# Gate products beside an RWKV scan without empty steps, and adaLN weights in four column groups

## The chip, the cores and the metric

The kernel runs on one core of a Trainium2 chip, in one launch. The metric is the device time of that launch in microseconds (us): the median of three runs, and beside it one execution that the hardware profiler recorded. The engines are TensorE (PE, with its weight loads PEld), VectorE (DVE), ScalarE (ACT), GpSimd (POOL) and SyncE (SP, which here issues most of the DMAs). All data are float32.

## The reference, cut to what matters

Two layers of a diffusion backbone over 256 context tokens and 512 latent tokens, 1024 wide. In the second layer (the last) only the latent tokens are carried on.

```python
def hybrid_layer(x, ctx, c, c_ctx, ...):
    shift, scale, gate = split(silu(c) @ ada_w + ada_b, 3)       # adaLN: 1024 x 3072, for c and for c_ctx
    p = split_cols(modulate(x, shift, scale) @ in_w, IN_SPLITS)  # one wide projection
    outs = [mla(p) * silu(p[3]),                                 # four mixers, each with its own gate
            rwkv(p) * silu(p[5]),                                # scan over the tokens, both ways
            gqa(p) * silu(p[9]),
            diff_attn(p) * silu(p[13])]
    g = sigmoid(p[14] + merge_b)                                 # 4 x 1024 merge gates: the widest part of in_w
    y = sum(g[i] * (outs[i] @ branch_w[i]) for i in range(4))
    return post_norm(ALPHA * x + gate * (y @ out_w), ln_g, ln_b)

def rwkv_step(S, r, w, k, v, kk, a):                             # per token and head, S is 64 x 64
    S = S * w - (S @ kk) * (kk * a) + v * k
    return S, S @ r
```

## The kernel before

**How a product is made.** Matmuls of the wide projection are made in three float32r passes: a weight block is split into a rounded part and the rest (`w_split`, L280: DMA at L292, the rounded part on ACT at L293, the difference on DVE at L296), and `mm3` (L299, matmul at L303) adds hi·hi, hi·lo and lo·hi. The blocks hold 1024 columns in a pool `wx` of five buffers; a block needs three of them, one for the raw weights and one for each part.

**Stages.** In us of the profiled span: the adaLN of layer 0 (0 to 45); the projections and the three attentions of layer 0 (45 to 592); its RWKV scan beside the gate products (592 to 988); its branch merges (988 to 1112); its output projection, with the last adaLN blocks of layer 1 (1112 to 1215); then the same for layer 1: attention to 1630, scan 1630 to 1965, merges to 2058, output to the end.

**The scan.** `rwkv_scan` (L1077) is a generator whose every step ends in a `yield`. It goes over six groups of two chunks of 64 tokens. `rwkv_prepare` (L1145) makes a group's matrices: products with `wup` and `aup` (L1167), G and the like (L1242, L1254, with DVE's L1246), and then an inverse in levels. A level is one dependent chain over two engines: DVE transposes D into tmp (L1290), 32 matmuls of 32x32 (L1295), DVE scales (L1298), 32 matmuls (L1319), DVE adds to D (L1320). `rwkv_chunks` (L1348) carries the state along (L1364, L1378, L1389, L1399).

**The gate products beside it.** `out_gate` and `late_gate` (through `m_block`) and `merge_gates` (through `t_block`) are a second generator, `rest`. For layer 0 it works on 768 tokens in two cuts of 384, for layer 1 on 512 in one. After every second of eight weight rows a block yields, so a step holds six matmuls of `mm3`. Before a block begins, `take_w` (L492) yields once with no work issued, and again as long as `wbusy` says that another generator is in the midst of a weight block. The gate products end in ACT's tanh (L1442), or in `gate` (L1413), where DVE's L1416 frees the PSUM buffer.

**What sets the order.** PE's order is that in which the program issues (`manual_schedule`); the other engines' orders come from the scheduler's priorities. `beside` (L203) runs the scan and, after each of its steps, as many steps of `rest` as `RATE[l]` (L36) has become due: 2.37 a step for layer 0, 1.3 for layer 1. Ahead of the scan `LEAD[2]` = 6 steps of `rest` are run; what is left of it comes after the scan. A step without work counts like any other.

```python
due = 0.0
for w in first:
    due += rate * (1.0 if w is None else w)
    while due >= 1:
        due -= 1
        next(second, None)
```

**adaLN.** `ada` (L376) multiplies the two conditioning vectors by 1024x3072 weights in six blocks of 512 columns a layer. A block comes in four pieces of 128x1024, each one DMA (L388). A matmul (L392) takes 128 rows of weights as its moving side, and writes 32 rows of PSUM: the row chunk i uses the array's column group i % 4. After the fourth piece ACT copies the sums (L397) and a small product adds up the four groups (L400). Layer 0's blocks 0 to 3 stand at the start; its blocks 4 and 5 and layer 1's 0 to 3 are filler in layer 0's attention; layer 1's 4 and 5 stand in layer 0's output projection.

**The tail.** `rwkv_finish` (L1100) normalizes the scan's output in two head pairs (PE transposes L1119 and L1121, DVE from L1125 to L1142). `merge` (L1447) multiplies each branch by its weights, transposes at L600, and DVE joins the products with the gates (L1480, L1483).

Of the kernel before, what the change touches and what calls it, by code (L numbers as in the profile page):

```python
# [18 lines left out]
DEPTH = 2  # L19
# [15 lines left out]
LEAD = (6, 1, 6)  # L35
RATE = (2.37, 1.3)  # L36
FILL = ((0.7, 0.65, 0.9), (0.5, 0.4, 0.5))
# [116 lines left out]
def _prep(inp):  # L154

    g = {k: np.asarray(v) for k, v in inp.items()}
    f = {}
    f["xin"] = np.concatenate([g["ctx"][0], g["x"][0]], 0)
    f["cc"] = np.stack([g["c_ctx"], g["c"][0]], -1).reshape(8, 128, 2).transpose(1, 0, 2).reshape(128, 16)
    order = [x for j in range(8) for x in (8 + j, j)] + list(range(16, 24))  # L160
    ada = g["ada_w"].reshape(DEPTH, 4, 2, 128, 24, 128)[:, :, :, :, order].reshape(DEPTH, 4, 2, 128, 6, 512)
    f["adaw"] = ada.transpose(0, 3, 4, 1, 2, 5).reshape(DEPTH, 128, 24 * 1024)
    brw = g["branch_w"].reshape(DEPTH, 4, 2, 128, 8, 128).transpose(0, 3, 1, 4, 2, 5).reshape(DEPTH, 128, 32, 256)
# [49 lines left out]
class _Kernel:  # L213
    def __init__(self, ctx, tc, a, out, tap):
# [14 lines left out]
        self.fp = None  # L229
        self.wbusy = False  # L230
        self.flip2 = 0

# [143 lines left out]
    def ada(self, l, ad, pp, pool, blocks, ahead=None):  # L376

        nc = self.nc
        for b in blocks:
            ps = self.P("A")  # L380
            for q in range(4):
                c = (b * 4 + q) * 1024
                if ahead is None:
                    yield from self.take_w()
                    w = self.t(self.fp, [128, 1024], "wf", bufs=2) if self.fp is not None else self.t(self.wp, [128, WCOLS], "wx", bufs=WBUFS)
                else:
                    w = self.t(ahead[0], [128, 1024], "adaw", bufs=ahead[1])
                nc.sync.dma_start(out=w[:, :1024], in_=self.a["adaw"][l][:, c:c + 1024])  # L388
                for k in range(2):
                    i = 2 * q + k  # L390

                    nc.tensor.matmul(ps[32 * (i % 4):32 * (i % 4) + 32], lhsT=self.cc[:, 2 * i:2 * i + 32], rhs=w[:, k * 512:k * 512 + 512],  # L392
                                     start=i < 4, stop=i >= 4)
                self.wbusy = False
                yield
# [96 lines left out]
    def take_w(self):  # L492

        yield
        while self.wbusy:
            yield
        self.wbusy = True
# [1035 lines left out]
def _run_layers(K, only=None):  # L1533
# [18 lines left out]
    for l in range(DEPTH):  # L1552
# [50 lines left out]
        if only == "attn":  # L1603
            return
        K.fp = None
        left = ExitStack()
        xct.close()
# [15 lines left out]
        with K.psum(A=(1, 2), B=(1, 3), C=(1, 2), Y=(1, 1)):  # L1623
# [14 lines left out]
            with mk(f"mg{l}") as K.mp:  # L1638
# [30 lines left out]
                gates_ = {s: K.gate_rows(ad, s) for s in ((1,) if last else (0, 1))}  # L1669
                run(tail)  # L1670
        with K.psum(A=(1, 8)):
            ys = K.out_operands(y, len(qt) * 128)
# [54 lines left out]
```

## Time and profile before

| | us |
|---|---|
| median of three runs | 2113.36 |
| lowest and highest | 2112.68 and 2114.27 |
| profiled execution | 2116.16 |
| its span, from the first to the last instruction | 2114.4 |
| PE busy | 1916.1 (91%) |
| PEld busy | 1579.2 (75%) |
| DVE busy | 1159.4 (55%) |
| ACT busy | 818.3 (39%) |
| POOL busy | 184.6 (9%) |
| mean granted PE clock | 0.958 |

The profiled execution takes 1.8 us more than its span, and 2.8 us more than the median. A float32 matmul leaves two records in the trace, an fp32r matmul one. Matmuls are pipelined and their ends are modelled, so a start to the next start says more than a duration. The gate products (L303 from `wx`) alone are 691.8 us of PE.

### The profile page before, as it was taken

The numbers are of one execution on the slowest core, as the hardware profiler recorded it, in microseconds if no ns is written. First come the engines' busy times: TensorE is split into PE (matmuls) and PEld (weight loads), VectorE is DVE, ScalarE is ACT, GpSimd is POOL, SyncE is SP. The second block draws the span as 40 slices with busy tenths as digits, with TensorE's granted clock in tenths as the row PEclk, the third lists the DMA queues.
The fourth block names the chain that finished last, engine by engine and source line by source line (L and its number), as shares of the span: only waits on it lengthen the run. The fifth ranks groups of instructions, "written<-read, shape, count | busy, mean of one in ns | idle before, by whom it ended". The sixth has DMA issues, their size and how long they took to land. (4 is left out here: it accounts for less than half of the span.)

```text
span 2114.4 us, 45822 instructions
## 1 busy us (share of the span) xinstructions
PE 1916.1 (91%) x19694; PEld 1579.2 (75%) x19694; DVE 1159.4 (55%) x2471; ACT 818.3 (39%) x1649; POOL 184.6 (9%) x303
## 2 busy tenths in 40 slices
PE   6899999988899999999788779999988988989877
PEld 4778868666788888888677577878877766766656
DVE  5554453576434434343778855454785444444677
ACT  3354452565323333232122336463664333332320
POOL 1000000001200000000230110001011000000120
PEclk9899999999899999999999989999999999999989
DMA  7110132220222222224642310101103222222741
GB/s 274 40 31 28 55 91 90 73 69 21 64 84 72 71 72 72 72 78 144 225 145 102 126 36 21 53 31 51 31 21 96 79 77 67 78 71 77 253 151 40
DMA packets 62612, 176.02 MB, mean 83 GB/s; under 512 B 7448, under 2 KB 12232, under 8 KB 62408
## 3 DMA queue, kind: packets, MB, share of 16 engines
q1 hardware_dynamic: 47144, 139.93, 21.0%
q10 hardware_dynamic: 13824, 27.90, 3.7%
q0 software_dynamic: 1440, 5.24, 0.6%
q8 instruction: 155, 2.54, 0.5%
q14 instruction: 49, 0.40, 0.1%
HBM read 145.50 MB, written 27.55 MB: 82 GB/s over the span
## 5 line engine op out<-in xcount | busy, mean ns | idle before, releaser
L303 PE MATMUL ps<-xh,wx 128*128 128x384 f32 (+2 forms) x3096 | 691.8, 369 | 1.5 <-DVE oth L1416 0.6
L303 PEld LDWEIGHTS ps<-xh,wx 128*128 128x128 f32 x3096 | 536.6, 190 | 64.0 <-issue 6.2
L293 ACT ACTIVATE wx<-wx 128x1024 fp32r<-128x1024 f32 (+2 forms) x94 | 98.2, 1045 | 307.3 <-PE ps L303 223.9
L296 DVE TENSOR_TENSOR wx<-wx,wx 128x1024 fp32r<-128x1024 f32 (+2 forms) x94 | 113.7, 1210 | 134.2 <-ACT wx L293 133.5
L649 DVE TENSOR_REDUCE nmax<-ps 128x1 f32<-128x768 f32 (+1 forms) x160 | 134.8, 847 | 64.3 <-PE ps L646 63.3
L571 PE MATMUL ps<-wx,xh 128*128 128x256 f32 (+1 forms) x1200 | 155.4, 288 | 7.7 <-DVE mu L1000 6.7
L571 PEld LDWEIGHTS ps<-wx,xh 128*128 128x128 f32 x1200 | 151.1, 191 | 9.4 <-ACT xc L476 6.8
L303 PE MATMUL ps<-xh,wb 128*128 128x384 f32 (+1 forms) x576 | 133.4, 384 | 27.1 <-DVE th L1482 19.3
L538 PE MATMUL ps<-wx,xh 128*128 128x256 f32 x960 | 140.3, 299 | 12.8 <-DVE oth L1416 6.3
L652 ACT ACTIVATE E<-ps,nmax 128x768 f32<-128x768 f32 (+1 forms) x160 | 130.5, 817 | 47.1 <-DVE nmax L649 42.9
L646 PE MATMUL ps<-qk,qk 128*128 128x384 f32 (+1 forms) x504 | 131.3, 366 | 17.3 <-ACT E L652 16.9
L303 PEld LDWEIGHTS ps<-xh,wb 128*128 128x128 f32 x576 | 108.0, 202 | 49.4 <-DVE th L1482 17.6
L538 PEld LDWEIGHTS ps<-wx,xh 128*128 128x128 f32 x960 | 129.3, 202 | 18.5 <-DVE oth L1416 6.5
L670 ACT ACTIVATE PH<-ps 128x512 f32<-128x512 f32 x156 | 91.4, 597 | 72.4 <-PE ps L668 71.8
L646 PEld LDWEIGHTS ps<-qk,qk 128*128 128x128 f32 x504 | 82.4, 192 | 45.0 <-ACT E L652 29.7
L668 PE MATMUL ps<-cstalways,E 128*128 128x128 f32 x624 | 102.3, 287 | 2.8 <-ACT PH L670 1.6
L1442 ACT ACTIVATE mth<-ps,hmb 128x384 f32<-128x384 f32 (+1 forms) x96 | 58.6, 610 | 118.6 <-PE ps L303 118.2
L693 PE MATMUL ps<-PH,V 128*64 128x256 f32 x624 | 85.7, 402 | 4.3 <-ACT PH L670 4.1
L668 PEld LDWEIGHTS ps<-cstalways,E 128*128 128x128 f32 x624 | 76.7, 147 | 16.8 <-ACT PH L670 4.3
L628 DVE TENSOR_TENSOR qk<-ps,qk 32x256 fp32r<-32x256 f32 (+5 forms) x104 | 59.3, 575 | 43.4 <-ACT qk L627 41.6
L296 DVE TENSOR_TENSOR wx<-wf,wx 128x1024 fp32r<-128x1024 f32 (+2 forms) x34 | 40.0, 1177 | 60.5 <-PE ps L303 33.8
L693 PEld LDWEIGHTS ps<-PH,V 128*64 128x64 f32 x624 | 41.0, 140 | 37.0 <-ACT PH L670 15.1
(325 smaller groups left out, 2799.9 us busy)
## 6 DMA issues: line engine op xcount, KB each, us to landing
wx<-in_inw_dram SPq DMA_DIRECT2D x88, 512.0 KB, 3.7
wf<-in_inw_dram SPq DMA_DIRECT2D x30, 512.0 KB, 3.6
wf<-in_adaw_dram SPq DMA_DIRECT2D x24, 512.0 KB, 3.6
gd<-mth ACTq DMA_DIRECT2D x32, 384.0 KB, 2.4
th<-gd SPq DMA_DIRECT2D x32, 384.0 KB, 3.1
adaw<-in_adaw_dram SPq DMA_DIRECT2D x16, 512.0 KB, 10.2
wx<-in_outw_dram SPq DMA_DIRECT2D x16, 512.0 KB, 6.2
wb<-in_brw_dram SPq DMA_DIRECT2D x32, 256.0 KB, 3.6
```

The source lines that it names most:

```text
L293: nc.scalar.activation(out=hi[:, :n], in_=raw[:, :n], func=AF.Copy)
L296: eng.tensor_tensor(out=lo[:, :n], in0=raw[:, :n], in1=hi[:, :n].bitcast(F32), op=ALU.subtract)
L303: self.nc.tensor.matmul(o, lhsT=w, rhs=x[:, s] if s is not None else x, start=first and p == 0, stop=last and p == 2)
L538: self.nc.tensor.matmul(ps[:, j * n:j * n + n], lhsT=self.xtok(x[k], s), rhs=w, start=k == 0 and p == 0 and j == 0, stop=k == 7 and p == 2 ...
L571: self.nc.tensor.matmul(ps, lhsT=self.xtok(x[k], s), rhs=w[:, c], start=k == 0 and p == 0 and head, stop=k == 7 and p == 2 and (tail or t ...
L628: nc.vector.tensor_tensor(out=lo[r, s], in0=ps[r], in1=hi[r, s].bitcast(F32), op=ALU.subtract)
L646: nc.tensor.matmul(o, lhsT=qt[:n, q], rhs=kt[:n, s], start=i == 0, stop=i == len(passes) - 1)
L649: nc.vector.tensor_reduce(out=nm, in_=v, axis=AX.X if ctx else AX.XY, op=ALU.max, negate=True)
L652: nc.scalar.activation(out=self.halves(e[:, :n], v), in_=v, func=AF.Exp, bias=nm, accum_out=den)
L668: nc.tensor.transpose(pt[:, c:c + 128], e[:, (k0 + k) * 128:(k0 + k) * 128 + 128], self.ident)
L670: nc.scalar.activation(out=hi, in_=pt, func=AF.Copy)
L693: nc.tensor.matmul(po[64 * (kk % 2):64 * (kk % 2) + 64, :n], lhsT=v2(kk), rhs=x[:, s], start=j == 0 and k < 2, stop=j == len(groups) - 1 a ...
```

## The change

Two edits that have nothing to do with each other.

First, a flag `eager` is set from the end of the attention to the output projection of each layer. While it is set, `take_w` does not yield first; it still yields as long as `wbusy` is set. A block of merge gates has 8 steps instead of 9 in layer 0, and 4 instead of 5 in layer 1; all gate products together 278 instead of 312, and 142 instead of 176. The rates go from 2.37 to 2.15 and from 1.3 to 1.08, so that with the scan's 126 steps of weight 277.0 and 142.1 steps are given out (304.6 and 169.8 before).

Second, an adaLN piece of 1024 columns holds four row chunks by 256 columns instead of two row chunks by 512. Each piece is four matmuls of 256 columns, one on each column group, instead of two of 512 on two groups. The layout of the weights in memory follows it. Bytes, DMAs and sums are the same.

```diff
-RATE = (2.37, 1.3)
+RATE = (2.15, 1.08)
...
-    ada = g["ada_w"].reshape(DEPTH, 4, 2, 128, 24, 128)[:, :, :, :, order].reshape(DEPTH, 4, 2, 128, 6, 512)
-    f["adaw"] = ada.transpose(0, 3, 4, 1, 2, 5).reshape(DEPTH, 128, 24 * 1024)
+    ada = g["ada_w"].reshape(DEPTH, 2, 4, 128, 24, 128)[:, :, :, :, order].reshape(DEPTH, 2, 4, 128, 6, 2, 256)
+    f["adaw"] = ada.transpose(0, 3, 4, 5, 1, 2, 6).reshape(DEPTH, 128, 24 * 1024)
...
-        self.wbusy = False
-        self.flip2 = 0
+        self.wbusy = self.eager = False
...
                 nc.sync.dma_start(out=w[:, :1024], in_=self.a["adaw"][l][:, c:c + 1024])
-                for k in range(2):
-                    i = 2 * q + k
-
-                    nc.tensor.matmul(ps[32 * (i % 4):32 * (i % 4) + 32], lhsT=self.cc[:, 2 * i:2 * i + 32], rhs=w[:, k * 512:k * 512 + 512],
-                                     start=i < 4, stop=i >= 4)
+                half = q // 2 * 256
+                for k in range(4):
+                    i = 4 * (q % 2) + k
+
+                    nc.tensor.matmul(ps[32 * k:32 * k + 32, half:half + 256], lhsT=self.cc[:, 2 * i:2 * i + 32],
+                                     rhs=w[:, k * 256:k * 256 + 256], start=q == 0, stop=q == 3)
                 self.wbusy = False
                 yield
...
     def take_w(self):
 
-        yield
+        if not self.eager:
+            yield
         while self.wbusy:
             yield
         self.wbusy = True
...
         K.fp = None
+        K.eager = True
         left = ExitStack()
...
                 run(tail)
+        K.eager = False
         with K.psum(A=(1, 8)):
```

Where a name in the rows below ends in a number, the number tells one buffer from another. The lines of the new kernel are one lower between L232 and L391, and one higher behind.

On PE, in a group's levels in layer 1's scan, before: the last matmuls of a gate block (L303), a level's second half (L1319), and the first half of the next level (L1295) with nothing between them.

```order
L303 MATMUL ps_18390<-xh_13199,wx_18385 128x512
L303 MATMUL ps_18390<-xh_13201,wx_18385 128x512
L303 MATMUL ps_18390<-xh_13199,wx_18386 128x512
L1319 MATMUL ps_18486<-D_18261,tmp_3153_18478 32x32 x32
L1295 MATMUL ps_18525<-tmp_3156_18523,G_3119_18166 32x32 x2
L1295 MATMUL ps_18525<-tmp_3156_18523,G_3120_18167 32x32 x2
```

The same place in the changed kernel.

```order
L302 MATMUL ps_18591<-xh_13147,wx_18587 128x512
L1320 MATMUL ps_18598<-D_18363,tmp_3153_18580 32x32 x32
L302 MATMUL ps_18591<-xh_13172,wx_18586 128x512
L302 MATMUL ps_18591<-xh_13174,wx_18586 128x512
L302 MATMUL ps_18591<-xh_13172,wx_18587 128x512
L302 MATMUL ps_18591<-xh_13198,wx_18586 128x512
L302 MATMUL ps_18591<-xh_13200,wx_18586 128x512
L302 MATMUL ps_18591<-xh_13198,wx_18587 128x512
L1296 MATMUL ps_18640<-tmp_3160_18638,G_3124_18278 32x32 x2
```

Six gate matmuls now stand between the two halves. Before, 13 pairs of scan steps in layer 1 had nothing between them, 75 stretches of gate matmuls held six, 22 twelve and one 72, and 36 gate matmuls came behind the scan; now no pair is empty, 96 stretches hold six, 16 twelve and one 48, and none comes behind the scan. In layer 0, 18 stretches held six matmuls, 58 twelve and 30 eighteen; now none holds six, 95 twelve and 12 eighteen, and behind the scan are 24 in place of 54. Around L1058, L1167 and L1242 ahead of layer 1's scan stood 36, 36 and 72 gate matmuls, now 48, 48 and 48. At eleven of the block ends in layer 1 DVE's split of the next weights comes in its order right ahead of an add or a scaling of the scan.

On PE, at the end of layer 1's scan, before: the output's transposes (L1119, L1121) of `rwkv_finish`, and 36 gate matmuls, of which the first three and the last stand here, ahead of the first merge (L600).

```order
L1119 MATMUL ps_21976<-cstalways_113,YT_17248 128x128 x4
L1121 MATMUL ps_21977<-cstalways_113,ks_17249 128x128 x4
L303 MATMUL ps_21868<-xh_13134,wx_21863 128x512
L303 MATMUL ps_21868<-xh_13136,wx_21863 128x512
L303 MATMUL ps_21868<-xh_13134,wx_21864 128x512
...
L303 MATMUL ps_21926<-xh_13199,wx_21922 128x512
L600 MATMUL ps_22013<-cstalways_113,O_14713 128x128 x4
```

The same place in the changed kernel.

```order
L302 MATMUL ps_21987<-xh_13291,wx_21983 128x512
L1120 MATMUL ps_22072<-cstalways_113,YT_17381 128x128 x4
L1122 MATMUL ps_22073<-cstalways_113,ks_17382 128x128 x4
L601 MATMUL ps_22109<-cstalways_113,O_14809 128x128 x4
L601 MATMUL ps_22118<-cstalways_113,O_14809 128x128 x4
L1113 MATMUL ps_22125<-ks_17382,cstrwkv_17279 128x512
```

The merge's transposes follow the finish's directly. On DVE the steps of the first head pair's finish now alternate with those of the first merge, where they stood ahead of it.

On PE, in layer 0's attention, before: an adaLN piece (`wf`, L392) between the scores (L646), transposes (L668, L600) and another piece.

```order
L646 MATMUL ps_2811<-qk_2450,qk_2414 128x384 x2
L392 MATMUL ps_2783<-wf_2822,cs_118 32x512 x2
L668 MATMUL ps_2826<-cstalways_113,E_2745 128x128
...
L600 MATMUL ps_2835<-cstalways_113,Qs_1997 128x128 x2
L392 MATMUL ps_2783<-wf_2862,cs_118 32x512 x2
```

The same place in the changed kernel.

```order
L647 MATMUL ps_2843<-qk_2482,qk_2446 128x384 x2
L392 MATMUL ps_2815<-wf_2854,cs_118 32x256 x4
L669 MATMUL ps_2860<-cstalways_113,E_2777 128x128
...
L601 MATMUL ps_2869<-cstalways_113,Qs_2029 128x128 x2
L392 MATMUL ps_2815<-wf_2896,cs_118 32x256 x2
```

A piece is four matmuls of half the width, and sometimes the scheduler cuts it in two. The 48 matmuls of 512 columns that are filler in the attention stood in 27 runs (13 of two, 10 of one, 4 of three), 17 of them between 284 and 394 us and 10 between 394 and 440; now 96 matmuls of 256 stand in 29 (15 of four, 6 of three, 2 of two, 4 of one, 2 of five).

## Rows read from the trace of the kernel before

**Rows 1.** Busy by stage: from:to, us, busy (instructions) per engine, granted clock, DMA share, GB/s.
```profile
284.00:394.00 110.00, 109.64 (x787) 85.93 (x786) 41.83 (x82) 44.34 (x96) 7.61 (x7) 1.00 0.29 88
394.00:440.00 46.00, 39.81 (x187) 21.17 (x188) 33.97 (x74) 30.93 (x71) 0.78 (x3) 0.85 0.43 127
592.00:988.00 396.00, 391.03 (x6539) 348.36 (x6536) 156.11 (x325) 123.06 (x260) 18.87 (x47) 1.00 0.23 74
1630.00:1965.00 335.00, 308.68 (x5675) 230.74 (x5674) 150.06 (x306) 110.25 (x229) 19.30 (x43) 0.97 0.25 76
1965.00:2058.00 93.00, 71.37 (x295) 52.32 (x294) 72.17 (x122) 26.57 (x41) 22.50 (x18) 0.93 0.67 221
```

**Rows 2.** PE's waits in layer 1's scan: waited for, us in total, times, longest.
```profile
PE ps L1319 <- DVE tmp L1298: 6.7, 7, 1.9
PE ps L1295 <- DVE tmp L1290: 5.6, 3, 2.4
...
PE ps L303 <- DVE oth L1416: 0.6, 1, 0.6
```

**Rows 3.** PE in time in layer 1's scan: start, us, instruction, records, [idle before].
```profile
1694.67 0.74 PE L1295 MATMUL ps<-tmp,G 32*32 32x32 f32 x64 [2.39 <-DVE tmp L1290]
...
1697.62 3.08 PE L303 MATMUL ps<-xh,wx 128*128 128x512 f32 x12
1700.63 0.75 PE L1295 MATMUL ps<-tmp,G 32*32 32x32 f32 x64
1701.31 1.67 PE L303 MATMUL ps<-xh,wx 128*128 128x512 f32 x6
1702.91 0.75 PE L1319 MATMUL ps<-D,tmp 32*32 32x32 f32 x64
1706.05 0.74 PE L1295 MATMUL ps<-tmp,G 32*32 32x32 f32 x64 [2.39 <-DVE tmp L1290]
```

**Rows 4.** DVE in time under the last wait of the group above.
```profile
1703.87 1.23 DVE L296 TENSOR_TENSOR wx<-wx,wx 128x1024 fp32r<-128x1024 f32 x1 [2.02 <-ACT wx L293]
1705.01 0.41 DVE L1320 TENSOR_TENSOR D<-D,ps 128x256 f32<-128x256 f32 x1
1705.46 0.45 DVE L1290 STREAM_TRANSPOSE tmp<-D 128x256 f32<-128x256 f32 x1
```

**Rows 5.** Busy in two of five stretches of layer 1's scan at half clock.
```profile
1707.40:1710.60 3.20, 3.20 (x9) 2.49 (x8) 0.00 (x0) 0.00 (x0) 0.00 (x0) 0.50 0.22 84
...
1929.30:1932.50 3.20, 3.20 (x70) 2.65 (x62) 0.87 (x2) 0.00 (x0) 0.00 (x0) 0.50 0.69 203
```

**Rows 6.** PE in time in layer 0's attention, at adaLN pieces (L392).
```profile
309.92 1.06 PE L392 MATMUL ps<-wf,cs 128*32 128x512 f32 x6
310.91 1.51 PE L693 MATMUL ps<-PH,V 128*64 128x256 f32 x12
```

**Rows 7.** PE in time between the layers, a dense adaLN block.
```profile
1197.04 1.92 PE L392 MATMUL ps<-wx,cs 128*32 128x512 f32 x16 [1.91 <-DVE ada L404]
```

**Rows 8.** Busy in two stretches, the instructions of L392 alone: PE, PEld, clock, DMA.
```profile
284.00:394.00 110.00, 17.86 (x60) 2.42 (x60) 1.00 0.29 88
394.00:440.00 46.00, 13.40 (x36) 1.74 (x36) 0.85 0.43 127
```

**Rows 9.** PE in time at the head of layer 1's scan.
```profile
1610.62 1.22 PE L1167 MATMUL ps<-wd,wup 64*128 64x128 f32 x8 [4.69 <-DMA kd<-kt]
...
1624.77 1.11 PE L1242 MATMUL ps<-KR,BK 64*128 64x64 f32 x16
```

**Rows 10.** DVE in time at the same place.
```profile
1623.94 0.42 DVE L1222 TENSOR_TENSOR KR<-kkn,P 128x256 f32<-128x256 f32 x1
```

**Rows 11.** PE in time behind layer 1's scan.
```profile
1965.47 8.69 PE L303 MATMUL ps<-xh,wx 128*128 128x512 f32 x36
```

**Rows 12.** Busy in the same 8.5 us and in the first merge behind them.
```profile
1965.50:1974.00 8.50, 8.50 (x39) 6.79 (x38) 5.97 (x19) 2.59 (x4) 0.87 (x1) 1.00 0.96 330
1974.00:1993.00 19.00, 15.41 (x71) 11.13 (x69) 14.04 (x34) 4.95 (x9) 1.92 (x2) 1.00 0.73 234
```

**Rows 13.** Costliest groups: line, engine, shapes, count, busy, mean ns, idle before.
```profile
L293 ACT ACTIVATE wx<-wx 128x1024 fp32r<-128x1024 f32 (+2 forms) x94 | 98.2, 1045 | 307.3 <-PE ps L303 223.9
```

## The prediction, made before the changed kernel was run

> **What bounds the kernel now.** I read the busy time by stage first [rows 1], because an average over stages with different limits says nothing of one edit. The five stages shown are those that the change touches. In the first of them, most of layer 0's attention, TensorE (PE) is busy 109.64 of 110 us: whatever is taken from PE's own work there is taken from the time. In the next 46 us PE has 39.81 at a mean granted clock of 0.85, with VectorE (DVE) at 33.97 and ScalarE (ACT) at 30.93: PE and the softmax chain take turns. The scan of layer 0 beside the gate products is PE's again (391.03 of 396). The scan of layer 1 is not: 308.68 of 335, which leaves 26.3 us of idle PE and a clock of 0.97. In the merges of layer 1 DVE is busy longer than PE (72.17 against 71.37).
>
> Second, who is waited for in layer 1's scan [rows 2]. The two largest are the scan's own small matmuls waiting for DVE between two of its steps; a gate matmul waits once, 0.6 us, and for the buffer of the gate before it, not for weights. Third, one such wait close up [rows 3, 4]. A step's 64 records (L1319) go out, nothing of the gates stands behind them, and the next step (L1295) starts 2.39 us later. In between DVE first finishes the split of the next weights (L296, 1.23), then adds and transposes (L1320, L1290). Where six gate records stand between two steps, PE has 1.60 us of work (1701.31 to 1702.91). The empty steps thus cost most when DVE has a split ahead of the scan's own work.
>
> Fourth, the granted clock. Five waits of 1.6 to 2.4 us in this stage are each followed within 4 us by at least 3.2 us at 0.50, the 1.2 GHz level; two of the five stretches stand in [rows 5]. Six other waits of 1.1 to 2.4 us are not followed by one (the 2.39 us before 1694.67 in [rows 3] is the nearest), so the loss does not go with the wait's length alone.
>
> **The change part by part.** *The adaLN pieces.* In the attention the products of 512 columns on 32 of the array's columns stand in 27 runs between other matmuls, most of one piece. A run of three matmuls (six records, since one float32 matmul leaves two) has 0.99 us from its start to the next start [rows 6], and eight matmuls spread on all four column groups take 1.92 [rows 7]. So matmuls on different groups lie beside each other, and the time is that of the fullest group: 0.96 for 512 columns. A piece of two matmuls uses two groups only and pays 0.96; a piece of four matmuls of 256 columns uses all four and should pay 0.48. The new order has 29 runs, two of them with a fifth matmul that repeats a group. I take 0.55 for a run (0.48, and 0.07 for an entry that a shorter run hides less, the difference between the 1.06 and the 0.99 of that row) and 0.48 more for each of the two. By [rows 8] the product costs 17.86 us of PE in the first stretch and 13.40 in the second (1.34 a run, part of it at half clock). Of the 17 runs of the first, 17.86 becomes some 10.5: 7.3 us gained in full, since PE is never idle there. Of the 10 of the second, 13.40 becomes some 8; I count less than half of that, 2.2, because the softmax chain holds PE there as well. **−9.5 us**, between −4 (half of the first stretch alone) and −13 (both in full). At the start and between the layers the pieces come in dense blocks of eight matmuls, which cost 1.92 in either form; **−1** there for a last piece that arrives late and is then done in half the time, 0 to −1.5.
>
> *No empty steps: layer 0.* The rule gives 277 of 278 filled steps in place of 305 of 312 with 34 empty ones. In the new order no scan step is left without matmuls behind it. PE's idle time there is 4.97 us [rows 1], all of it waits for DVE after short or empty fills; **−4.5**, 0 to −5.
>
> *Layer 1's head.* Now all six leading steps are full, so the gate products before the scan's first matmuls shift: the runs around L1058, L1167 and L1242 go from 36, 36 and 72 matmuls to 48, 48 and 48. The wait of 4.69 us before L1167 [rows 9], for a transfer, is covered by 12 matmuls more (3 us). But L1242 cannot start before KR, which DVE finishes at 1624.36 [rows 10], and the total ahead of it is the same: what is hidden first reappears at L1242, and moving the work earlier may push DVE's gate step (L1416) in front of it. **+1.5**, 0 to +3.
>
> *Layer 1's scan.* All 13 pairs of steps with nothing between them are filled; runs of six gate matmuls go from 75 to 96, and the longest from 72 to 48. Of the 26.3 us of idle time I leave 9. Eleven block ends still fall right before a step that DVE has to finish behind a split: five leave 0.8 (2.39 less the 1.60 of a run of six) and four some 0.25, 5 in all, and the waits for G at L1254 and the like, 4, are the scan's own chain. That is **−17**. The five half-clock stretches last 16 us and do 8 us' work; every one follows a wait that is filled now: **−8**. Against that stand 14 more runs. A run of twelve lasts 3.01 (1697.62 to the next start in the trace at 1700.63) and two of six 3.20, so an entry costs 0.19, in all **+2.8**. Together **−22**, from −12 (the clock is not given back and half of the waits return) to −28.
>
> The rule of the Trainium skill that speaks against this part is in "TensorEngine Tiling (Array Packing)", section Key Properties: changing the tiling mode, not merely the tile, drains the engine, and the new order changes it 28 times more. The page gives no price; were a change free, the sum would be 2.8 lower, and by the 0.19 of the row, which agrees with the rule, it is the one used.
>
> *Layer 1's tail.* In the old order 36 gate matmuls, 8.69 us [rows 11], come after the scan's last step, and under them DVE does 5.97 us of the finish of the first head pair [rows 12]. They are inside the scan now and fill its gaps, which is counted above. The 5.97 us of DVE are left without that cover: they land beside the first merge, where DVE already has 14.04 of 19 us. 14.04 + 5.97 is 20.0, a little over the 19 that this stretch takes; with the order of a chain that alternates between engines **+4**, 0 to +8.
>
> Sum: −9.5 −1 −4.5 +1.5 −22 +4 = −31.5. From the profiled execution of 2116.16 us that is 2084.7. The median of the three runs is 2113.36, 2.8 lower, so **2082 us**.
>
> **The rivals.** *A, the wait takes the place.* The empty step gave DVE time for the split of the new weights. If at each of the 32 block ends of layer 1's scan the split now stands in front of the scan's add, each costs 0.8 us as above, 25 us of waits in place of 26; only the clock's 8 and the other terms stay. The sum is −14.5, **2099 us**. For it: the split lasts 1.23 and is not moved by the change [rows 4]. Against it: the new order has such a place at eleven ends, not at all 32.
>
> *B, the adaLN gain is hidden.* If the softmax chain on DVE and ACT ends last in the attention, shorter products only make PE wait. −2 in place of −9.5: **2089.5 us**. Against it stands 109.64 of 110; for it, that a busy PE in the profile is modelled from pipelined matmuls and need not be at its peak.
>
> *C, slower: the weights come late.* With the empty step gone the first gate matmul of a block follows the last of the block before at once. Should each of the 66 blocks (34 a layer, less the first of each) wait for its split weights, the change loses from 0.48 us a block on (31.5 / 66), and at 1 us a block the time is 2113.4 −31.5 +66 = **2148 us**. Against it: no gate matmul waits for weights now [rows 2], a block has 335 / 32 = 10.5 us, and what comes after a buffer is free is ACT's 1.05 [rows 13] and DVE's 1.23; the DMA share is 0.25.
>
> *D, A and B together* with the tail at its upper end: −14.5 +7.5 +4 = −3, **2110 us**, no difference that shows. That the empty steps do not go, because the weights are marked busy and the loop still yields, the new order excludes.
>
> The clock may also stay low. Of its five falls three come behind a wait of 1.63 to 1.82 us, and the waits I leave are 0.8: if the falls stay, 8 us come back, 2090. "TensorE: Matmul & The Clock Gate", section "What's actually happening", in the Trainium skill says that activity releases the throttle; by it fuller gaps mean fewer falls, and the six waits here without a fall neither prove nor deny it.
>
> **How the numbers follow.** The forecast has a chance of 0.60; B or the clock alone 0.16, A 0.15, D 0.05, C 0.04. With all terms at their good ends (−13, −1.5, −5, 0, −28, 0) the sum is −47.5, 2066; that all are good at once I hold for unlikely, and the low end is 2068. At the high end the range takes in A and a little more, 2101, and leaves out D, C and 0.06 of A's and the forecast's own tails. A measurement of this kernel tells about 0.2% from no change, 4.2 us. Faster by more than that are the forecast, A and B, 0.91; within it D, 0.05; slower C, 0.04.
>
> **What would show it.** In the profile after, idle PE in layer 1's scan should be near 9 us and its clock near 1.00; the runs of L392 in the attention some 0.55 us and the first attention stretch some 7 us shorter; layer 0's scan without idle time; the stretch from the scan's end to the second merge about 4 us longer than its PE work. The forecast is wrong if waits for the add behind the split come at most block ends (A), if PE shows new idle time before softmax-fed matmuls (B), or if gate matmuls wait for the split weights (C).

## The result and the profile after

| | before | changed | ratio, 95% interval |
|---|---|---|---|
| median, first chip | 2113.02 us | 2084.55 us (2079.98 to 2086.42) | 0.9864 (0.9848 to 0.9879) |
| again, another chip | 2112.63 us | 2083.71 us (2078.71 to 2089.62) | 0.9862 (0.9842 to 0.9882) |
| profiled execution | 2116.16 us | 2084.66 us | |
| its span | 2114.4 us | 2082.9 us | |

The change makes the kernel 28.5 us faster by the medians and 31.5 by the two profiled executions. The prediction was 2082 us, and a sum of −31.5.

Stages are compared below from the same event to the same event. These are L571's first matmul, two starts of the scores (L646), L1058, the first L1242, the first merge transpose (L600), and so on. The columns are those of [rows 1]: stretch, length, busy (records) of PE, PEld, DVE, ACT and POOL, granted clock, DMA share, GB/s. Before: the first part of layer 0's attention, layer 0's scan from its first L1242 to the merge, layer 1's from its first L1295 to the merge, and from there to the last L600.

```profile
249.90:395.20 145.30, 144.80 (x1011) 114.10 (x1010) 60.47 (x118) 64.20 (x141) 7.84 (x10) 1.00 0.25 76
582.60:997.00 414.40, 409.43 (x6677) 366.10 (x6677) 164.66 (x340) 127.58 (x266) 18.87 (x47) 1.00 0.25 79
1636.80:1974.00 337.20, 311.52 (x5669) 233.93 (x5668) 152.44 (x317) 109.66 (x227) 20.16 (x44) 0.97 0.26 82
1974.00:2037.70 63.70, 46.28 (x187) 33.01 (x185) 48.68 (x80) 16.88 (x25) 15.64 (x14) 0.92 0.75 246
```

The same four stretches of the changed kernel, and behind the first the rest of layer 0's attention up to L1058, which took 149.1 us before.

```profile
248.00:387.20 139.20, 138.69 (x1066) 114.60 (x1066) 59.89 (x117) 62.74 (x139) 7.83 (x10) 1.00 0.26 77
387.20:537.20 150.00, 128.12 (x868) 99.16 (x868) 104.74 (x230) 91.41 (x201) 10.66 (x17) 0.90 0.18 53
573.30:985.40 412.10, 408.78 (x6665) 364.83 (x6665) 163.82 (x339) 127.34 (x265) 18.72 (x47) 1.00 0.25 78
1624.90:1942.00 317.10, 306.12 (x5668) 226.82 (x5667) 146.62 (x299) 107.80 (x225) 17.89 (x43) 1.00 0.26 82
1942.00:2007.70 65.70, 49.05 (x188) 34.65 (x186) 52.24 (x99) 17.78 (x28) 16.15 (x14) 0.90 0.75 253
```

Two thirds of the gain lie in layer 1's scan: 337.2 to 317.1 us, although the gate matmuls that stood behind it ([rows 11]) are counted in both. Its idle PE goes from 25.7 to 11.0 us (length less busy), and its granted clock from 0.97 to 1.00; no stretch at 1.2 GHz is left in it. Where [rows 2] had 6.7, 5.6 and more, the waits of PE in layer 1's scan are now these (what is waited for: us in total, times, longest; "issue" is a wait for which the trace names no cause).

```profile
PE ps L1296 <- DVE tmp L1291: 3.2, 4, 0.8
PE ps L1320 <- issue: 2.4, 3, 1.1
PE ps L302 <- issue: 1.4, 2, 1.2
...
PE ps L1306 <- DVE tmp L1291: 0.8, 1, 0.8
PE ps L1320 <- DVE tmp L1299: 0.7, 3, 0.2
```

Five waits of 0.79 us and three of 0.23 stand at block ends, where the prediction had five of 0.8 and four of 0.25. One of them on PE and then on DVE (start, duration, instruction, records, idle time before), beside [rows 3, 4]:

```profile
1788.92 0.75 PE L1320 MATMUL ps<-D,tmp 32*32 32x32 f32 x64
1789.60 1.67 PE L302 MATMUL ps<-xh,wx 128*128 128x512 f32 x6
1792.06 0.80 PE L1296 MATMUL ps<-tmp,G 32*32 32x32 f32 x64 [0.79 <-DVE tmp L1291]
```

```profile
1789.88 1.22 DVE L295 TENSOR_TENSOR wx<-wx,wx 128x1024 fp32r<-128x1024 f32 x1 [2.01 <-ACT wx L292]
1791.02 0.41 DVE L1321 TENSOR_TENSOR D<-D,ps 128x256 f32<-128x256 f32 x1
1791.47 0.45 DVE L1291 STREAM_TRANSPOSE tmp<-D 128x256 f32<-128x256 f32 x1
```

The split of the next weights (L295, 1.22 us) still stands ahead of the scan's add, but six gate matmuls now cover 1.6 of the 2.39 us. For the adaLN products alone the two stretches that answer to [rows 8] are these (PE, PEld, clock, DMA), and one run on PE with its follower stands behind them, beside [rows 6]:

```profile
282.00:386.80 104.80, 12.23 (x120) 3.18 (x120) 1.00 0.31 91
386.80:430.50 43.70, 7.86 (x72) 1.77 (x72) 0.90 0.47 142
```

```profile
301.09 0.64 PE L392 MATMUL ps<-wf,cs 128*32 128x256 f32 x8
301.66 0.44 PE L647 MATMUL ps<-qk,qk 128*128 128x384 f32 x1
```

### The profile page after: what moved, and what is told of

Read it like the earlier page. It is cut to its first block, busy times and chain, and to the rows that moved or that the text cites. A ratio compares the mean times of both kernels' runs of the same rounds, so it can differ in the third digit from the quotient of the medians.

```text
span 2082.9 us, 46213 instructions
## 1 busy us (share of the span) xinstructions
PE 1903.6 (91%) x19886; PEld 1575.2 (76%) x19886; DVE 1156.1 (56%) x2471; ACT 816.6 (39%) x1649; POOL 181.2 (9%) x303
## 5 line engine op out<-in xcount | busy, mean ns | idle before, releaser
L295 DVE TENSOR_TENSOR wx<-wx,wx 128x1024 fp32r<-128x1024 f32 (+2 forms) x94 | 113.5, 1208 | 143.9 <-ACT wx L292 143.3
L539 PE MATMUL ps<-wx,xh 128*128 128x256 f32 x960 | 139.9, 299 | 14.5 <-DVE oth L1417 7.4
L647 PE MATMUL ps<-qk,qk 128*128 128x384 f32 (+1 forms) x504 | 134.8, 371 | 16.7 <-ACT E L653 16.4
L1443 ACT ACTIVATE mth<-ps,hmb 128x384 f32<-128x384 f32 (+1 forms) x96 | 58.6, 611 | 113.1 <-PE ps L302 111.5
L295 DVE TENSOR_TENSOR wx<-wf,wx 128x1024 fp32r<-128x1024 f32 (+2 forms) x34 | 40.0, 1178 | 60.4 <-PE ps L302 33.8
L694 PEld LDWEIGHTS ps<-PH,V 128*64 128x64 f32 x624 | 41.8, 143 | 36.5 <-ACT PH L671 14.1
## 6 DMA issues: line engine op xcount, KB each, us to landing
adaw<-in_adaw_dram SPq DMA_DIRECT2D x16, 512.0 KB, 10.2
```

The costliest lines, as they stand in the source:

```text
L295: eng.tensor_tensor(out=lo[:, :n], in0=raw[:, :n], in1=hi[:, :n].bitcast(F32), op=ALU.subtract)
L539: self.nc.tensor.matmul(ps[:, j * n:j * n + n], lhsT=self.xtok(x[k], s), rhs=w, start=k == 0 and p == 0 and j == 0, stop=k == 7 and p == 2 ...
L647: nc.tensor.matmul(o, lhsT=qt[:n, q], rhs=kt[:n, s], start=i == 0, stop=i == len(passes) - 1)
L694: nc.tensor.matmul(po[64 * (kk % 2):64 * (kk % 2) + 64, :n], lhsT=v2(kk), rhs=x[:, s], start=j == 0 and k < 2, stop=j == len(groups) - 1 a ...
```

## The experiments

All were compared with the kernel before on the chip on which they ran. The medians scatter by 3 us or so, and stages that an edit does not touch differ from profile to profile (the second part of layer 0's attention took 148.3 to 153.5 us in kernels with the same adaLN pieces). So the small effects are read by stages. In us, from the same events as above (half clock is time at the 1.2 GHz level; the last column is called the tail):

| kernel | ratio to before (interval) | attention, first part | layer 1's scan | idle PE in it | half clock in it | to the last merge transpose |
|---|---|---|---|---|---|---|
| before | 1 | 145.3 | 337.2 | 25.7 | 17.1 | 63.7 |
| changed | 0.9864 (0.9848 to 0.9879) | 139.2 | 317.1 | 11.0 | 0 | 65.7 |
| changed, again | 0.9862 (0.9842 to 0.9882) | 139.3 | 317.2 | 10.9 | 0 | 65.7 |
| adaLN pieces alone | 0.9939 (0.9925 to 0.9953) | 139.3 | 336.9 | 24.5 | 20.5 | 61.7 |
| no empty steps alone | 0.9891 (0.9873 to 0.9909) | 145.3 | 315.6 | 9.5 | 3.4 | 67.7 |
| old rates | 0.9973 (0.9960 to 0.9986) | 139.3 | 324.5 | 20.5 | 17.1 | 62.1 |
| empty steps in mid-block | 0.9883 (0.9865 to 0.9901) | 139.2 | 321.5 | 16.6 | 3.4 | 60.8 |
| empty steps, split on POOL | 0.9879 (0.9856 to 0.9901) | 139.3 | 323.2 | 17.2 | 6.8 | 58.9 |
| all splits on POOL | 0.9906 (0.9891 to 0.9921) | 139.3 | 313.5 | 7.2 | 3.4 | 65.9 |
| split in halves | 0.9860 (0.9843 to 0.9877) | 139.2 | 315.9 | 9.8 | 0 | 63.6 |
| tail kept | 0.9864 (0.9846 to 0.9883) | 139.2 | 323.5 | 13.6 | 10.2 | 60.9 |
| 24 splits on POOL | 0.9857 (0.9836 to 0.9879) | 139.3 | 313.9 | 7.5 | 3.4 | 65.6 |
| 24 splits on POOL, tail kept | 0.9826 (0.9807 to 0.9844) | 139.3 | 309.6 | 4.9 | 0 | 59.2 |
| adaLN products twice | 0.9875 (0.9854 to 0.9897) | 145.3 | 314.0 | 8.5 | 0 | 66.0 |

**The changed kernel once more**, on the chip of three of the experiments below.

> The changed kernel itself once more, beside the three that follow and on the same chip, as their measure: 2082 to 2088 us. By stages, where layer 0's attention from its second half on and the spans between the layers differ by some us from execution to execution, layer 1's scan should be 317 us from its first L1296 to the merge's first L601, and the way from there to the last L601 66 us.

2083.71 us, and the two stages as expected: 317.2 and 65.7 us. These two repeat to the tenth between two chips; the spread of the total comes from elsewhere.

**The two parts alone.** The adaLN edit with `take_w` and the rates of before, and the other way round.

```diff
-RATE = (2.15, 1.08)
+RATE = (2.37, 1.3)
...
-        if not self.eager:
-            yield
+        yield
```

> The adaLN pieces of four column groups alone; steps, rates and gate products as before. The theory (an adaLN run costs its fullest column group, and PE sets the end of most of the attention): 2 us at the start and 5 to 8 in layer 0's attention, so 2103 to 2106 us. The rival that the softmax chain hides the attention's part: 2110 us or more, only the start's 2 us.

> No empty steps and the new rates alone; the adaLN pieces as before. The theory: 4.5 us in layer 0's scan and about 20 in layer 1's from its head to its first merge, so 2087 to 2091 us, with idle PE of 11 us and the clock at 1.00 in layer 1's scan. If the two parts help each other (the clock, the places of transfers), this and the run of the pieces alone would not add up to the change's 28.5 us; the theory says that they do, within 3 us.

Medians of 2100.03 and 2090.59 us beside 2114.08 on that chip: −14.1 and −23.5. The gain of the first part shows where it was expected, in the first part of the attention, and nothing of it in the scan:

```profile
246.80:386.10 139.30, 138.80 (x1066) 114.69 (x1066) 59.94 (x118) 62.66 (x140) 7.82 (x10) 1.00 0.26 77
1627.70:1964.60 336.90, 312.44 (x5669) 234.82 (x5668) 151.81 (x316) 109.55 (x227) 19.25 (x43) 0.97 0.26 81
```

The second part alone shows the reverse:

```profile
248.00:393.30 145.30, 144.80 (x1010) 114.14 (x1009) 60.44 (x118) 64.15 (x141) 7.82 (x10) 1.00 0.26 76
1631.60:1947.20 315.60, 306.11 (x5668) 227.43 (x5667) 146.53 (x299) 107.67 (x225) 17.17 (x43) 0.99 0.26 82
```

The medians add up to 37.5 us where the change has 28.5, further off than the 3 us that were expected. The second part alone lies in its range, the first 3 us below its own. In the stages that the parts touch they do add up (145.3, 139.3, 139.2; and 336.9, 315.6, 317.1). Most of the rest came from stages that neither touches: in the profile of the pieces alone, layer 1's merges and its end after the scan take 5 us less than before. Why that kernel had so much there was not settled; its clock in these stretches differs from profile to profile in all kernels.

**The rates.** The changed kernel with the old ones.

```diff
-RATE = (2.15, 1.08)
+RATE = (2.37, 1.3)
```

> The changed kernel with the old rates 2.37 and 1.3: no empty steps, but the gate products run out 11 scan steps early in layer 0 and 21 steps early in layer 1, where the last group has eight pairs of half levels and the last chunks with nothing between them. The theory (a scan step without gate matmuls leaves PE 1.2 to 1.9 us idle): 21 steps of 1.5 us in layer 1 and 11 of 1.2 in layer 0 are 45 us, less 25 entries of 0.19 that go, so about 2120 us, slower than before. The rival that the empty steps alone cost, and the rates only have to be high enough: 2085 us.

2108.23 us (0.9973): some 23 us worse than the change, but not the 35 expected. Where the gate products have run out, in layer 1's last group, PE's chain of levels stands bare:

```profile
1942.50 0.26 PE L1296 MATMUL ps<-tmp,G 32*32 32x32 f32 x8 [1.09 <-DVE tmp L1291]
...
1944.21 0.75 PE L1320 MATMUL ps<-D,tmp 32*32 32x32 f32 x64 [0.52 <-DVE tmp L1299]
...
1950.73 1.18 PE L1296 MATMUL ps<-tmp,G 32*32 32x32 f32 x64 [1.12 <-DVE tmp L1291]
```

In these levels a step without gate matmuls costs 0.52 or 1.09 us, not 1.2 to 1.9. No split of weights is left to be made at that point. From 1945 us on PE runs at half clock for 17 us (the last of these rows takes 1.18 us in place of 0.74), so a fall of the clock can follow a row of short waits too. So the price expected was that of an empty step with a split in it. Without the fitted rates four fifths of the change's gain are lost all the same, and not mainly at that place: in layer 1 the way from L1059 to the last merge transpose is 7.9 us longer than in the changed kernel, and in layer 0 the way from L1059 to the first product of layer 1 is 12.5 us longer, 7.8 of them in the merges and the output. What makes those longer was not looked into.

**Empty steps away from the split.** One empty step put back in each of layer 1's merge-gate blocks, in its middle.

```diff
-RATE = (2.15, 1.08)
+RATE = (2.15, 1.28)
...
                 if k % 2:
                     yield
+                if k == 3 and mode == "lat" and self.eager:
+                    yield
```

> The changed kernel with one empty step put back in layer 1, but in the middle of each block of merge gates, away from its end where DVE's split of the next weights lies, and a rate of 1.28 to fit; some 14 pairs of scan steps have nothing between them again. Theory 1 (an empty pair costs the scan's own chain on DVE, 1.6 us, and the half clock follows such a wait): 14 waits of about 1.6 and two or more falls of the clock, layer 1's scan 12 to 18 us longer than the changed kernel's, 2097 to 2103 us. Theory 2 (it was the split at the block's end that made the empty pairs dear): less than 6 us, 2090 or less.

2089.18 us, 5.5 above the changed kernel on the same chip (2083.71), with intervals that overlap: theory 2. Scan and tail together take 382.3 us beside 382.9, with six gate matmuls, 1.4 us, moved ahead of them. Eleven pairs of scan steps stand bare in the trace of this scan, where before had 13, but those in the levels cost what the old rates showed. Two of them on PE (L1322 and L1298 are L1319 and L1295 of before):

```profile
1639.06 0.75 PE L1322 MATMUL ps<-D,tmp 32*32 32x32 f32 x64 [0.52 <-DVE tmp L1301]
...
1746.55 0.74 PE L1298 MATMUL ps<-tmp,G 32*32 32x32 f32 x64 [1.09 <-DVE tmp L1293]
```

In before the first was up to 1.9 us and the second 2.4 ([rows 2, 3]).

**Empty steps with the split elsewhere.** The reverse: the empty steps and rates of before, where they were, and the split of the merge gates' weights on POOL.

```diff
-RATE = (2.15, 1.08)
+RATE = (2.37, 1.3)
...
-        hi, lo = self.w_split(self.a["inw"][l][:, off:off + 8 * n], 8 * n)
+        hi, lo = self.w_split(self.a["inw"][l][:, off:off + 8 * n], 8 * n,
+                              eng=self.nc.gpsimd if mode == "lat" and name[:2] == "mg" else None)
...
-        if not self.eager:
-            yield
+        yield
```

> The empty steps and the rates of the kernel before, the adaLN pieces as changed, and the split of layer 1's merge gates on POOL. The theory that the empty pairs were dear because DVE's split lay in them: the waits of 1.87 and 2.39 us fall to 0.52 and 1.09, the half clock in layer 1's scan goes down from 17 to 20 us to under 10, and that scan from 337 to 320 to 326 us, 2087 to 2092 in all. The rival that an empty pair costs as such, whatever DVE has: 332 us or more there, 2098 to 2102.

2086.77 us (0.9879), and layer 1's scan 323.2 us in place of the 336.9 of the kernel that differs by the split alone. Its stretch and one bare step:

```profile
1627.70:1950.90 323.20, 306.04 (x5670) 230.52 (x5667) 132.60 (x287) 109.53 (x227) 90.20 (x74) 0.99 0.27 86
```

```profile
1686.18 0.89 PE L1296 MATMUL ps<-tmp,G 32*32 32x32 f32 x64 [1.09 <-DVE tmp L1291]
```

2.39 ([rows 3], and the same in the adaLN pieces alone) has become 1.09. With nothing else moved, 13.7 of the 20 us in layer 1's scan are had, and the half clock goes from 20.5 to 6.8 us, although three waits of 1.8 to 3.7 us are new; in the longest DVE is held beside POOL, as told below. The two runs together show what made the empty steps dear: DVE's 1.2 us split in front of the scan's add, at a place where PE had nothing. The empty step itself is not free. Scan and tail together take 382.1 us here, where they took 398.6 with the split on DVE, but 379.5 and 368.8 in the two kernels below that have 24 blocks split on POOL and no empty steps.

**What is left in the changed kernel.** Three attempts at the five waits of 0.79 us. First the split of all gate blocks of layer 1 on POOL; `scan1` is set from the end of layer 1's attention until the gate products are done.

```diff
-            eng = nc.vector
+            eng = nc.gpsimd if self.eager and self.scan1 else nc.vector
```

> The changed kernel with the split of the gate weights in layer 1's scan on POOL in place of DVE. The theory (the waits that are left, five of 0.79 us and some of 0.2 to 0.7, stand where DVE's split lies ahead of the scan's add): they go, 5 to 7 us, so 2078 to 2080 us, provided that POOL splits a block within the 10 us that a block lasts. The rival that these waits are the scan's own chain: 2084.5. Should POOL's split be so late that the gate matmuls wait for their weights: above 2090.

2093.58 us (0.9906), worse than the change although its scan is 3.6 us shorter. It lies above 2090, but not for the reason given for that: no gate matmul is shown waiting for its weights in the scan. The waits of 0.79 are gone, and two new ones have come, of 1.8 us and this:

```profile
PE ps L1390 <- DVE SV L1385: 3.4, 1, 3.4
```

DVE was held there beside POOL's pass (its L1111 took 2.84 us in place of 0.74). The clearest case (DVE's row, then POOL's):

```profile
1729.68 2.62 DVE L1394 TENSOR_TENSOR S<-ssum,pe 128x256 f32<-128x256 f32 x1
```

```profile
1729.34 2.69 POOL L295 TENSOR_TENSOR wx<-wx,wx 128x1024 fp32r<-128x1024 f32 x1 [0.18 <-ACT wx L292]
```

L1394 takes 0.40 to 0.42 us where POOL has no such pass; here it ends 0.3 us behind POOL's (1732.3 and 1732.0). An operation that takes one of its operands from PSUM is not held, as this pair shows:

```profile
1922.11 0.42 DVE L1321 TENSOR_TENSOR D<-D,ps 128x256 f32<-128x256 f32 x1 [2.19 <-PE ps L1320]
```

```profile
1922.04 2.39 POOL L295 TENSOR_TENSOR wx<-wx,wx 128x1024 fp32r<-128x1024 f32 x1 [5.84 <-ACT wx L292]
```

The Trainium skill, "GPSIMD Engine Reference", section Specifications, lists POOL's SBUF interfaces as shared with VectorE, with contention for DVE instructions that have two SBUF inputs; these rows agree (L1394 has two, 2.62 us; L1321 has one and PSUM, 0.42). Outside the scan the profile is 13 us longer than the changed kernel's: 5.5 in layer 1's attention and 2.1 in the head, where the leading gates were split on POOL as well, and the rest in stages that the edit doesn't touch. So the second attempt leaves the leading gates and the last eight blocks to DVE.

```diff
-        hi, lo = self.w_split(self.a["inw"][l][:, off:off + 8 * n], 8 * n)
+        hi, lo = self.w_split(self.a["inw"][l][:, off:off + 8 * n], 8 * n,
+                              eng=self.nc.gpsimd if mode == "lat" and "mg" <= name < "mg3" else None)
```

> The changed kernel with the split of layer 1's first 24 blocks of merge gates on POOL (2.4 us each) in place of DVE; the last eight, which POOL would split beside the finish, and the gates before them stay on DVE. If the waits of 0.79 us are the split's, they go without the two long waits that the run with all blocks on POOL showed (3.4 and 1.8 us): layer 1's scan and the way to the last L601 together 376 to 380 us in place of 383, in all 2078 to 2082. If POOL slows DVE wherever the two overlap, by more than the waits are worth: 2085 or more.

2080.11 us (0.9857): scan and tail 379.5 us in place of 382.9, inside its range. Three waits of that kind are left (0.80 to 0.85 us), each at one of the blocks whose split stayed on DVE, and none at the others: so these waits are the split's. The total cannot be told from the changed kernel's. The third keeps DVE and cuts its split in two.

```diff
-        eng.tensor_tensor(out=lo[:, :n], in0=raw[:, :n], in1=hi[:, :n].bitcast(F32), op=ALU.subtract)
+        for c in ((slice(0, n // 2), slice(n // 2, n)) if self.scan1 else (slice(0, n),)):
+            eng.tensor_tensor(out=lo[:, c], in0=raw[:, c], in1=hi[:, c].bitcast(F32), op=ALU.subtract)
```

> The changed kernel with DVE's split of the gate weights of layer 1's scan in two instructions of half the width. If the waits that are left (five of 0.79 us, others of 0.2 to 0.7) come from the split's length ahead of the scan's add, they shrink by up to 0.6 us each and the scan gets 2 to 4 us shorter: 2081 to 2083. If the scheduler puts both halves at the same place, or another wait takes over, no change: 2084.5.

2082.09 us (0.9860): no change that can be told. The five waits shrink from 0.79 to 0.73 only, since the chain still has both halves ahead of it: one before the add, one between the add and the transpose (L1322 and L1292 in this kernel). On DVE at the second of them:

```profile
1788.52 0.69 DVE L296 TENSOR_TENSOR wx<-wx,wx 128x512 fp32r<-128x512 f32 x1 [2.01 <-ACT wx L292]
1789.13 0.41 DVE L1322 TENSOR_TENSOR D<-D,ps 128x256 f32<-128x256 f32 x1
1789.46 0.68 DVE L296 TENSOR_TENSOR wx<-wx,wx 128x512 fp32r<-128x512 f32 x1
1790.07 0.43 DVE L1292 STREAM_TRANSPOSE tmp<-D 128x256 f32<-128x256 f32 x1
```

**The tail.** A lower rate in layer 1: 42 gate matmuls behind the scan again, and no bare step.

```diff
-RATE = (2.15, 1.08)
+RATE = (2.15, 1.03)
```

> The changed kernel with a rate of 1.03 in layer 1: no pair of scan steps is empty, but 42 more gate matmuls stand behind the scan, as in the kernel before, above the finish of the first head pair. The theory of the tail (that finish lost its cover and now stands beside the first merge, 4 us): the way from the scan's end to the last L601, less the gate matmuls in it, is 2 to 4 us shorter, against which more runs of six leave 1 to 3 us more idle time in the scan; 2081 to 2085 in all. If the tail's cover is worth nothing: 2085 to 2088.

2083.35 us (0.9864), even. Both halves of the expectation show: to the last merge transpose it takes 60.9 us in place of 65.7, and the scan, which ends with the 42 matmuls, is 6.4 us longer, with idle PE of 13.6 and 10.2 us at half clock. Of the 4.8 us, 1.7 are the clock: 10.2 us of that way are at half clock, where the changed kernel has 13.7 (0.92 and 0.90 in the rows).

```profile
1626.40:1949.90 323.50, 309.86 (x5668) 229.64 (x5667) 151.22 (x316) 109.15 (x227) 21.20 (x45) 0.98 0.27 85
1949.90:2010.80 60.90, 45.93 (x187) 33.55 (x185) 49.05 (x81) 16.88 (x25) 14.70 (x13) 0.92 0.75 248
```

Both edits together, the lower rate and the split of 24 blocks on POOL:

> As the run with 24 blocks on POOL, and a rate of 1.03 in layer 1, so that 42 gate matmuls stand behind the scan above the finish, which took 5 us out of the way to the last L601 when it was tried with the split on DVE, and was lost again in the scan to waits of 0.8 to 1.8 us behind runs of six. With the split on POOL these waits should stay away: 374 to 379 us for scan and tail, 2076 to 2081 in all. If the longer runs of before were what hid them: 2083 or more.

2073.57 us (2072.07 to 2077.01), 0.9826 (0.9807 to 0.9844): faster than both kernels, and below the range of the expectation, as are scan and tail with 368.8 us. The lower rate's price in the scan is gone: idle PE is 4.9 us, where the tail kept with the split on DVE had 13.6, and nothing is left of 10.2 us at half clock.

```profile
1628.20:1937.80 309.60, 304.72 (x5668) 226.27 (x5667) 137.07 (x293) 108.79 (x226) 72.11 (x67) 1.00 0.28 90
1937.80:1997.00 59.20, 45.88 (x186) 32.94 (x185) 49.41 (x81) 16.80 (x25) 14.53 (x13) 0.91 0.77 255
```

**The adaLN price.** Each adaLN matmul in the attention twice.

```diff
-                for k in range(4):
-                    i = 4 * (q % 2) + k
...
+                reps = 2 if ahead is None and self.fp is not None else 1
+                for z in range(reps):
+                    for k in range(4):
+                        i = 4 * (q % 2) + k
...
```

> The changed kernel with each adaLN matmul that is filler in layer 0's attention issued twice, so that those blocks' sums come out twice as large; bytes and DMAs as before. Each of the 24 pieces gains 0.48 us of PE, some 15 of them in the first half of that attention and 9 in the second. If PE sets the end in the first half alone, and the softmax chain in the second: the first half goes from 139.2 to about 146.5 us, and the second stays within its own 148 to 153; 2090 to 2093 in all. If PE sets the end in both: 4 us more in the second half, 2095 to 2097. If the first half does not move, the adaLN gain of the change was not PE's time at all.

2088.95 us (0.9875), 2 to 3 us above the change by the ratios, which can hardly be told apart, and just below the range. The first part of the attention grows by 6.1 us (7.3 were expected), to the 145.3 that it has in the kernel before:

```profile
249.20:394.50 145.30, 145.08 (x1185) 118.20 (x1185) 60.30 (x117) 63.07 (x139) 7.82 (x10) 1.00 0.24 71
```

A run of eight matmuls, two on each column group, starts 1.00 us before its follower:

```profile
308.98 1.07 PE L394 MATMUL ps<-wf,cs 128*32 128x256 f32 x16
309.98 0.44 PE L696 MATMUL ps<-PH,V 128*64 128x256 f32 x2
```

So in the first part PE's work is the time, and the gain of that term is right in kind. The second part took 154.4 us, 0.9 above the longest of the others; whether the adaLN products weigh there at all stays open.

## Why the prediction was right, and where its terms were off

The time, 2082 us, was 2.6 us below the median, well inside the range, and the sum of −31.5 met the profiled execution to the tenth. Some of that is luck: the terms were off by up to 4.3 us, and cancelled, and by the medians the gain is 28.5.

- **Layer 1's scan, −22: −20.1.** Idle time was to go by 17 and went by 14.7; of the 11.0 us that are left 4.6 stand at the block ends (5 foreseen, right in number and size) and 2.4 in waits for G and the like (4 foreseen); the 3.9 marked "issue" were not foreseen. The clock came back in full (17.1 us at half clock to none, worth 8.5). PE's busy time fell by 5.4, so 3.1 us were added by other things, where the 14 more entries were to cost 2.8 (by the counts ahead of the prediction they are 15). Rival A named the right mechanism, a split ahead of the add, but at all 32 ends; of the eleven where the new order had it, eight show a wait, of the size that was said. (Its sum of −14.5 takes 25 us of waits as no gain on 26, which is 1 us too little.)
- **The tail, +4: +2.0, and not by the cause given.** DVE's busy time in that stretch did grow, by 3.6 us, but 1.7 of the 2.0 are the clock (13.7 us at half clock in place of 10.2), and PE's idle time there did not grow. Of the 5.97 us in [rows 12] some 1.4 were not the finish but the merge's own splits (L1472). The kernel that kept the tail has 60.9 beside 65.7, some 3 us at an equal clock; the profile of before had a long tail for its kind (63.7, where the other kernels with gate matmuls behind the scan had 58.9 to 61.7). The stretch behind the tail was 1.5 us shorter than before, which the edit of the steps alone does not show (76.7 there and before).
- **The attention, −9.5: −6.1 in its first part, nothing that shows in the second.** The first size was wrong at one step: 17.86 us is the sum of durations (1.05 a run), in which each overlaps its follower by 0.07, while the 0.55 was a start-to-start figure. From start to start 17 runs of 0.98 are 16.7 us, and the 18 that stand there now, two of them with a fifth matmul, 11.1: 5.6. The 2.2 of the second part were a guess. The adaLN products there did shrink by 5.5 us (13.40 to 7.86, in part because fewer ran at half clock), but the stretch to L1058 took 150.0 us in place of 149.1, so no gain shows there, as rival B has it.
- **Layer 0's scan, −4.5: −4.5, in two places.** 2.3 are in the scan; 2.2 come from its head, between L1058 and the first L1242 (38.3 to 36.1), which the working did not cost. A new wait of 1.7 us for ACT's tanh (L1443) took some of the scan's.
- **Layer 1's head, +1.5: −1.1.** The step that failed took KR's time as fixed. It is not: DVE had a split in the midst of that chain (first row, before), which in the changed kernel is done ahead of L1168 (second row), and the first L1243 follows L1168 by 8.4 us in place of 14.2 ([rows 9]), with 48 gate matmuls between them in place of 72. That the split freed the chain is argued from its place; its own length is 1.2 us of it. From L1058 to the first L1242 the head is 2.0 us shorter, and from there to the first L1295 0.9 longer.

```profile
1617.66 1.23 DVE L296 TENSOR_TENSOR wx<-wx,wx 128x1024 fp32r<-128x1024 f32 x1 [0.82 <-ACT wx L293]
```

```profile
1602.55 1.23 DVE L295 TENSOR_TENSOR wx<-wx,wx 128x1024 fp32r<-128x1024 f32 x1 [1.76 <-ACT wx L292]
```

- **The start, −1:** 43.0 to 41.8 us, but the pieces alone had 43.6 and the kernel with the old pieces 41.1, so this is not shown.
- **C and D** did not come: no gate matmul is shown waiting for its weights in layer 1's scan (two waits, 1.4 us in all, have no cause in the trace), and the attention's gain and the filled gaps are both there.

The prediction saw that an empty step is dearest where DVE has a split ahead of the scan's work. It took the 26 us of idle time from the trace and let most of it go, so it needed no price of the step itself. The expectations of the experiments did, and put it at 1.2 to 1.9 us a step. The runs say 0.52 or 1.09 for the step itself, and 1.3 more where a split of weights is queued ahead on DVE.

Open: what exactly makes the clock fall. In layer 1's scan the kernels whose longest wait was 1.33 us or less had no half clock; with the old rates a fall came behind a row of waits of up to 1.12, where the filler had run out; the kernels with waits of 1.74 us or more had 3.4 to 20.5 us of it; and of two waits of 1.36 us, in two kernels, one was followed by a fall and one was not. Not every long wait was followed by a fall, and no run varied the wait alone.

## What to carry to other kernels

A bubble on the busiest engine is dear through what another engine does in it: look at what stands ahead of the needed instruction in that engine's queue, and move that, as well as filling the bubble. When steps are handed out at a rate, fit the rate when empty ones are taken away: with the old one the filler ran out early here, and four fifths of the gain were lost. Filler moved forward may uncover work behind it. Work out a gain from start to start on both sides, never from durations on one side.

## What the runs showed of the hardware

POOL's pass over 128x1024 float32 (2.4 us) held a DVE operation with two SBUF operands that started after it until just behind its own end (2.62 us in place of 0.42), and did not slow one with a PSUM operand (0.42). The other overlaps in the four kernels with splits on POOL show the same. And a run of matmuls on 32 of the array's columns is paid by its fullest column group: from its start to the next, one to four matmuls of 256 columns on different groups took 0.55 to 0.57 us, and one to three of 512 on different groups 0.98 to 0.99; five of 256, with one group used twice, took 0.98, and eight, each group twice, 1.00. Doing each of them twice brought the first part of the attention back to the 145.3 us that it has with the pieces of 512.
